# Gated delta recurrence: the keys' roots on ScalarE's logarithm and exponential, the convolution's first product from SBUF

## The chip, the cores and the metric

The kernel runs on one core of a Trainium2 chip. The metric is the device time of one execution in microseconds (us); of several runs the median is taken. The engines of the core work side by side, each through its own list of instructions in order: TensorE (PE, matrix products; PEld is its weight load), VectorE (DVE), ScalarE (ACT), GpSimd (POOL) and SyncE (SP, which issues most of the DMA transfers). They wait for each other through semaphores. SBUF is the memory on the chip, and PSUM the small memory that TensorE writes its products to.

## What is computed

The reference is two transformer blocks one after the other, in float32, on 512 tokens of width 1024. The change touches the second block's gated delta network, in which queries and keys are brought to length one behind a convolution of five taps and a SiLU:

```python
def _gdn_inputs(qkv, beta_logit, decay_logit, conv_w, a_log, dt_bias):
    qkv = jax.nn.silu(_centred_conv(qkv, conv_w))
    ...
    q = _l2norm(q.reshape(B, T, GDN_HEADS, GDN_DK))
    k = _l2norm(k.reshape(B, T, GDN_HEADS, GDN_DK))
```

A recurrence in chunks of 128 tokens follows, forward and backward, over 256 context tokens and the 512 tokens themselves (six chunks), for 8 heads of width 128. Beside it the block has a latent attention (MLA), whose latents are a product of the same input, and an MLP.

## The kernel before

Float32 products are made from three matmuls of high and low parts (`mm3s`, L234, L235 and L237: high by high, low by high, high by low). `weights()` loads a chunk of weights of 512 KB (tile `wraw`), from which ScalarE makes the high part `whi` (L178) and VectorE the low part `wlo` (L179); the three names share six buffers. Products of the projections go to a PSUM bank of the group `pg`, of which there are two.

`gdn()` works through four pairs of heads. For each pair:

- `inputs(pair)` projects keys and queries. `conv()` takes each product out of its PSUM bank twice on ScalarE: L1247 copies it to `raw`, and L1248 writes it, scaled by the middle tap, to `acc`. VectorE adds the other four taps (L1254), and ScalarE applies the Silu (L1256). Each head's keys are turned (TensorE L1284, ScalarE L1286), and ScalarE squares them and sums (L1309, tile `kss`). GpSimd adds 1e-6 (L1312, tile `kn`), raises to the power -1/2 (L1314) and multiplies (L1315): the root of the keys' squared length, `krt`.
- `values(pair)` does the same for the values and scales them by `krt` as they leave PSUM (L1289).
- `betas(pair)` takes the logarithm of `kn` on ScalarE (L1344, tile `kln`) and its reciprocal on VectorE (L1346).
- `within(pair)` makes the matrices inside a chunk: TensorE L1368 to L1378, Exps on ScalarE (L1380), VectorE L1382 to L1384, and copies to the tile `inv` (L1388, L1390).
- `states(pair)` inverts them. VectorE transposes all blocks (L1398), eliminates (L1406, L1409) and transposes back (L1411 for one half, L1412 for the other). TensorE then puts larger blocks together (L1426 to L1466; ScalarE copies in L1437), and six steps of the recurrence follow (L1472 to L1535).
- `output(pair)` norms the result, multiplies it by a gate (Silu L1543, L1560) and stores it by a DMA that ScalarE issues (L1561).

In the code, `inputs`, `values`, `betas` and `within` of the next pair stand behind `states` of this one, and behind the last pair's `states` the products of the MLA latents (`tail()`: three chunks of 256, 256 and 192 columns, taken out of PSUM by L980). A scheduler orders the instructions of TensorE, ScalarE, VectorE and GpSimd when the kernel is built, so work of the next pair, or of the tail, is placed among the steps and the inversion of this one. SyncE keeps the written order. The scheduler's result depends on the whole program: a change of a few instructions can move others.

Of the kernel before, what the change touches and what calls it, by code (L numbers as in the profile page):

```python
# [10 lines left out]
F32 = mybir.dt.float32  # L11
F32R = mybir.dt.float32r
BF = mybir.dt.bfloat16
AF = mybir.ActivationFunctionType
OP = mybir.AluOpType
# [60 lines left out]
class Kernel:  # L76
# [1155 lines left out]
    def gdn(self, H, HC, w, tail):  # L1232
        nc, ap = self.nc, self.ap
        mm, act, dve = nc.tensor.matmul, nc.scalar.activation, nc.vector
        con = self.const
        sel, cw, onw, ones, idb, msk = self.sel, self.convw, self.onw, self.ones, self.idb, self.msk
        X, L, Y = (self.hb.tile([128, 32, 32], F32, name="inv", tag=f"inv{k}") for k in range(3))
        tm = [con.tile([128, 136], F32, name=f"invt{v}") for v in range(2)]
        nc.gpsimd.memset(X, 0.0)

        def conv(ps, tile):

            raw, acc = (self.page([sum(p.shape[1] for p in ps)]) for _ in range(2))
            o = 0
            for p in reversed(ps):
                n = p.shape[1]
                act(raw[:, o:o + n], p, AF.Copy)  # L1247
                act(acc[:, o:o + n], p, AF.Copy, scale=cw[:, 48 + tile:49 + tile])  # L1248
                for i in (0, 1, 3, 4):
                    wi = cw[:, 24 * i + tile:24 * i + tile + 1]  # L1250
                    a, b = max(0, 2 - i), min(n, n + 2 - i)
                    y = acc[:, o + a:o + b]
                    v = raw[:, o + a + i - 2:o + b + i - 2]
                    dve.scalar_tensor_tensor(y, v, wi, y, op0=OP.mult, op1=OP.add)  # L1254
                o += n
            act(acc, acc, AF.Silu)  # L1256
            return acc, raw

        def product(W, X, f, n, tag):
            ps = self.bank([128, n], tag)  # L1260
            self.mm3s(ps, [[v[:, f * 128:f * 128 + 128] for v in W[k]] for k in range(8)], X)
            return ps

        def ahead(f0):

            W = self.weights(w, 0, 8, f0, 256)
            return W, [product(W, HC, f, 256, "sc") for f in range(2)]

        def feat(f0, both, first=None):

            W, pc = first or (None, None)
            W = W or self.weights(w, 0, 8, f0, 256)
            for f in range(2):
                r = [product(W, H, f, 512, "pg")]
                if both:
                    r.append(pc[f] if pc else product(W, HC, f, 256, "pg"))
                yield r

        def turn(src, dst, scale=None):

            for a, m in ((0, 4), (4, 2)):
                pt = self.bank([128, m, 128], "pt")
                for t in range(m):
                    nc.tensor.transpose(pt[:, t], src[:, (a + t) * 128:(a + t) * 128 + 128], self.ident)  # L1284
                if scale is None:
                    act(dst[:, a:a + m], pt, AF.Copy)  # L1286
                    continue
                for t in range(m):
                    act(dst[:, a + t], pt[:, t], AF.Copy, scale=scale[:, a + t:a + t + 1])  # L1289
# [3 lines left out]
        def inputs(pair):  # L1293


            h0 = 2 * pair
            qT, sq_, kT, ktok = ([] for _ in range(4))
            fk = fv = None
            if pair == 0:
                fv = None, ahead(2048)[1]  # L1300
                fk = ahead(1024)
            kc = [conv(ps, 8 + h0 + f) for f, ps in enumerate(feat(1024 + pair * 256, True, fk))]
            n2, root = [], []
            for f, (c, raw) in enumerate(kc):
                kt = self.page([6, 128])
                turn(c, kt)
                ss = self.tmp.tile([128, 6], F32, name="kss")
                for t in range(6):
                    act(raw[:, t * 128:t * 128 + 128], kt[:, t], AF.Square, accum_out=ss[:, t:t + 1])  # L1309
                n2.append(self.hb.tile([128, 6], F32, name=f"kn2{f}", bufs=2))  # L1310
                root.append(self.hb.tile([128, 6], F32, name=f"krt{f}", bufs=2))
                nc.gpsimd.tensor_scalar(n2[f], ss, 1e-6, None, op0=OP.add)  # L1312
                r = self.hb.tile([128, 6], F32, name="krs", bufs=2)
                nc.gpsimd.tensor_tensor(r, n2[f], self.mhalf[:, :6], op=OP.pow)  # L1314
                nc.gpsimd.tensor_tensor(root[f], r, n2[f], op=OP.mult)  # L1315
                kT.append(c.rearrange("p (a b) -> p a b", a=6))
                ktok.append(kt)
            qc = [conv(ps, h0 + f) for f, ps in enumerate(feat(pair * 256, False))]
            for q, sq in qc:
                qT.append(q)  # L1320
                act(sq, q, AF.Square)
                pq = self.bank([128, 4], "pt")
                for t in range(4):
                    mm(pq[:, t:t + 1], sq[:, t * 128:t * 128 + 128], ones, start=True, stop=True)
                s1 = self.tmp.tile([128, 4], F32, name="qss")
                dve.tensor_copy(s1, pq)
                sq_.append(self.rstd(s1, 1.0 / 128, 128e-6, "qrs"))
            return (qT, kT, ktok), (root, sq_), n2, fv

        def values(pair, root, fv):  # L1330

            vtok = []
            for f, ps in enumerate(feat(2048 + pair * 256, True, fv)):
                c, _ = conv(ps, 16 + 2 * pair + f)
                vt = self.page([6, 128])
                turn(c, vt, root[f])
                vtok.append(vt)
            return vtok

        def betas(pair, n2):  # L1340
            h0, nb, bd = 2 * pair, [], []
            for f in range(2):
                ln = self.hb.tile([128, 6], F32, name="kln", bufs=2)
                act(ln, n2[f], AF.Ln)  # L1344
                inv = self.hb.tile([128, 6], F32, name="kin", bufs=2)
                dve.reciprocal(inv, n2[f])  # L1346
                for out, nm, v, op in ((nb, "nb", ln, OP.subtract), (bd, "bd", inv, OP.mult)):
                    out.append(self.hb.tile([128, 6, 2], F32, name=f"k{nm}{f}", bufs=2))
                    dve.tensor_tensor(out[f], g[nm][:, :, h0 + f::8], v[:, :, None].to_broadcast([128, 6, 2]), op=op)
            return nb, bd  # L1350

        D2 = range(2)
# [210 lines left out]

        gg = self.gdn_gates(H, HC, w)
        keys, rest, n2, fv = inputs(0)
        next(gg)
        vtok = values(0, rest[0], fv)
        next(gg)
        g = next(gg)
        nb, bd = betas(0, n2)  # L1570
        EM = within(0, *keys[:2], nb)
        for pair in range(4):
            O = states(pair, *keys, vtok, bd, *EM)
            sq_ = rest[1]
            if pair < 3:
                keys, rest, n2, fv = inputs(pair + 1)
                vtok = values(pair + 1, rest[0], fv)
                nb, bd = betas(pair + 1, n2)
                EM = within(pair + 1, *keys[:2], nb)
            else:  # L1580
                tail()
            output(pair, O, sq_)
# [54 lines left out]
```

## Time and profile before

| | us |
|---|---|
| median of 3 runs | 2291.25 (2290.05 to 2291.55) |
| the profiled execution | 2289.66 |
| its span | 2287.8 |
| TensorE busy | 2185.6 (96%) |
| VectorE busy | 1186.6 (52%) |
| ScalarE busy | 1019.1 (45%) |
| GpSimd busy | 259.3 (11%) |

The busy shares are means over the whole span. TensorE is idle for some 100 us in all, so it is the first engine to look at, and the question is at which places it waits and for whom. The granted clock is TensorE's, as a share of full speed; its mean was 0.984. The recurrence with its inputs and the tail fills the stretch from about 940 to 1460 us. In the timelines a row is one instruction, or several of a kind in a row (xN): its start, its duration, its engine, line and operation, what it writes and reads, and in brackets how long its engine had been idle before it and who released it.

### The profile page before, as it was taken

The page shows a single profiled execution, that of the slowest core. Times are in us where ns is not written, and L with a number is a line of the kernel's source. Part 1 is how long each engine was busy: PE and PEld are TensorE (multiplying, and loading weights), DVE is VectorE, ACT ScalarE, POOL GpSimd, SP SyncE. Part 2 cuts the span into 40 slices and gives each one's busy share as a digit, 9 for nine tenths or more (in the row PEclk, how much of TensorE's full clock was granted, in tenths as well). Part 3 has the DMA queues.
Part 4 walks back from the last instruction along what each step waited for, and adds up shares of the span by engine and source line. Part 5 has one row for each costly group of instructions (what it writes and reads, how often), then busy time and mean ns, then how long its engine had stood idle before and what let it go on. Part 6 is the DMA issues. An engine that isn't in the chain of part 4 may idle for free. (4 is left out here: it accounts for less than half of the span.)

```text
span 2287.8 us, 38189 instructions
## 1 busy us (share of the span) xinstructions
PE 2185.6 (96%) x15367; PEld 1938.3 (85%) x15367; DVE 1186.6 (52%) x2636; ACT 1019.1 (45%) x2072; POOL 259.3 (11%) x411
## 2 busy tenths in 40 slices
PE   7999999998999999998999998999999998999999
PEld 7888988888889889877787888789998797898988
DVE  3554453656443233558687875337774444424333
ACT  4443333545443223566665664446554224314231
POOL 0220100001000001203121211201110011010102
PEclk9999999999999999999999998999999998999999
DMA  5134476455773233522222110331013442223222
GB/s 169 65 115 145 156 245 225 153 184 177 256 248 105 90 102 102 165 81 66 74 66 79 61 56 16 98 117 34 30 38 111 166 144 78 93 90 95 93 92 102
DMA packets 195816, 262.05 MB, mean 115 GB/s; under 512 B 12343, under 2 KB 157495, under 8 KB 195639
## 3 DMA queue, kind: packets, MB, share of 16 engines
q1 hardware_dynamic: 188864, 244.61, 33.1%
q10 hardware_dynamic: 6775, 15.00, 1.7%
q8 instruction: 121, 1.98, 0.3%
q14 instruction: 56, 0.46, 0.1%
HBM read 223.39 MB, written 36.18 MB: 113 GB/s over the span
## 5 line engine op out<-in xcount | busy, mean ns | idle before, releaser
L179 DVE TENSOR_TENSOR wlo<-wraw,whi 128x1024 fp32r<-128x1024 f32 (+2 forms) x267 | 321.7, 1205 | 415.9 <-PE pg L235 213.4
L178 ACT ACTIVATE whi<-wraw 128x1024 fp32r<-128x1024 f32 (+2 forms) x267 | 276.8, 1037 | 443.6 <-DMA wraw<-in_w_mlp_out 96.2
L234 PE MATMUL pg<-xhi,whi 128*128 128x512 f32 (+1 forms) x1104 | 429.4, 391 | 26.7 <-ACT a L1248 15.9
L235 PE MATMUL pg<-xlo,whi 128*128 128x512 f32 (+1 forms) x1104 | 425.4, 388 | 0.0
L237 PE MATMUL pg<-xhi,wlo 128*128 128x512 f32 (+1 forms) x1104 | 293.7, 385 | 2.6 <-DVE wlo L179 2.6
L234 PEld LDWEIGHTS pg<-xhi,whi 128*128 128x128 f32 x1104 | 210.8, 191 | 74.8 <-ACT a L1248 18.1
L235 PEld LDWEIGHTS pg<-xlo,whi 128*128 128x128 f32 x1104 | 210.8, 191 | 37.1
L237 PEld LDWEIGHTS pg<-xhi,wlo 128*128 128x128 f32 x1104 | 203.1, 190 | 41.7 <-DVE wlo L179 3.3
L234 PE MATMUL pg<-whi,xhi 128*128 128x256 f32 (+1 forms) x608 | 160.5, 294 | 3.3 <-ACT whi L178 2.5
L235 PE MATMUL pg<-whi,xlo 128*128 128x256 f32 (+1 forms) x608 | 156.6, 288 | 0.0
L234 PE MATMUL sc<-whi,a 128*128 128x256 f32 x560 | 140.8, 283 | 1.6 <-ACT whi L178 1.6
L234 PE MATMUL pg<-whi,a 128*128 128x256 f32 x560 | 140.9, 283 | 0.5 <-DVE a L148 0.5
L235 PE MATMUL sc<-whi,a 128*128 128x256 f32 x560 | 141.1, 284 | 0.0
L235 PE MATMUL pg<-whi,a 128*128 128x256 f32 x560 | 140.8, 283 | 0.0
L234 PEld LDWEIGHTS pg<-whi,xhi 128*128 128x128 f32 x608 | 118.7, 195 | 10.2 <-ACT whi L178 4.4
L235 PEld LDWEIGHTS pg<-whi,xlo 128*128 128x128 f32 x608 | 118.2, 195 | 1.1 <-issue 0.8
L234 PEld LDWEIGHTS sc<-whi,a 128*128 128x128 f32 x560 | 107.4, 192 | 2.0 <-ACT whi L178 1.8
L234 PEld LDWEIGHTS pg<-whi,a 128*128 128x128 f32 x560 | 107.5, 192 | 0.9 <-DVE a L148 0.9
L1254 DVE SCALAR_TENSOR_TENSOR a<-a,convw,a 128x511 f32<-128x511 f32 (+3 forms) x160 | 97.7, 638 | 20.1 <-ACT a L1248 19.2
L235 PEld LDWEIGHTS sc<-whi,a 128*128 128x128 f32 x560 | 107.5, 192 | 0.2
L929 POOL TENSOR_TENSOR a<-a,a 128x256 f32<-128x256 f32 x64 | 48.8, 763 | 519.5 <-DVE a L928 518.8
L235 PEld LDWEIGHTS pg<-whi,a 128*128 128x128 f32 x560 | 107.5, 192 | 0.0
(475 smaller groups left out, 4570.4 us busy)
## 6 DMA issues: line engine op xcount, KB each, us to landing
wraw<-in_w_in SPq DMA_DIRECT2D x56, 512.0 KB
fraw<-in_w_mod SPq DMA_DIRECT2D x48, 512.0 KB
parts<-fraw SPq DMA_DIRECT2D x48, 512.0 KB
wraw<-in_w_gate_up SPq DMA_DIRECT2D x44, 512.0 KB
wraw<-in_w_mlp_in SPq DMA_DIRECT2D x32, 512.0 KB
wraw<-in_w_mlp_out SPq DMA_DIRECT2D x32, 512.0 KB
whi<-parts SPq DMA_DIRECT2D x26, 512.0 KB
wlo<-parts SPq DMA_DIRECT2D x26, 512.0 KB
```

Source lines behind the costliest of these rows:

```text
L178: nc.scalar.activation(hi, raw, AF.Copy)
L179: self.wlo_eng.tensor_tensor(lo, raw, hi.bitcast(F32), op=OP.subtract)
L234: mm(out, A[k][0], B[k][0], start=start and k == 0, stop=False)
L235: mm(out, A[k][late], B[k][1 - late], start=False, stop=False)
L237: mm(out, A[k][1 - late], B[k][late], start=False, stop=stop and k == n - 1)
L929: nc.gpsimd.tensor_tensor(self.x[t][:, cs], self.x[t][:, cs], u, op=OP.add)
L1254: dve.scalar_tensor_tensor(y, v, wi, y, op0=OP.mult, op1=OP.add)
```

## The change

`conv()` makes the second eviction from `raw` in SBUF and not from PSUM, so that the bank is free after the first. The three GpSimd instructions on the keys of each head go; instead ScalarE takes one logarithm for both heads of a pair, with 1e-6 as its bias, and the exponential of half of it, which is the root. `betas()` uses the same logarithm; VectorE adds 1e-6 and takes the reciprocal of both heads at once. From L1241 on lines of the kernel after stand up to three further down: L1247 and L1248 are L1250 and L1251 there, the keys' Ln and Exp are L1315 and L1317, and the lines from L1348 on keep their numbers.

```diff
+        eps = con.tile([128, 1], F32, name="keps")
+        nc.gpsimd.memset(eps, 1e-6)
...
                 act(raw[:, o:o + n], p, AF.Copy)
-                act(acc[:, o:o + n], p, AF.Copy, scale=cw[:, 48 + tile:49 + tile])
+                act(acc[:, o:o + n], raw[:, o:o + n], AF.Copy, scale=cw[:, 48 + tile:49 + tile])
...
-            n2, root = [], []
+            ss = self.hb.tile([128, 2, 6], F32, name="kss", bufs=2)
...
-                ss = self.tmp.tile([128, 6], F32, name="kss")
                 for t in range(6):
-                    act(raw[:, t * 128:t * 128 + 128], kt[:, t], AF.Square, accum_out=ss[:, t:t + 1])
-                n2.append(self.hb.tile([128, 6], F32, name=f"kn2{f}", bufs=2))
-                root.append(self.hb.tile([128, 6], F32, name=f"krt{f}", bufs=2))
-                nc.gpsimd.tensor_scalar(n2[f], ss, 1e-6, None, op0=OP.add)
-                r = self.hb.tile([128, 6], F32, name="krs", bufs=2)
-                nc.gpsimd.tensor_tensor(r, n2[f], self.mhalf[:, :6], op=OP.pow)
-                nc.gpsimd.tensor_tensor(root[f], r, n2[f], op=OP.mult)
+                    act(raw[:, t * 128:t * 128 + 128], kt[:, t], AF.Square, accum_out=ss[:, f, t:t + 1])
...
+            ln = self.hb.tile([128, 2, 6], F32, name="kln", bufs=2)
+            act(ln, ss, AF.Ln, bias=eps)
+            root = self.hb.tile([128, 2, 6], F32, name="krt", bufs=2)
+            act(root, ln, AF.Exp, scale=0.5)
...
-                turn(c, vt, root[f])
+                turn(c, vt, root[:, f])
...
+            ss, ln = n2
+            inv = self.hb.tile([128, 2, 6], F32, name="kin", bufs=2)
+            dve.tensor_scalar(inv, ss, 1e-6, None, op0=OP.add)
+            dve.reciprocal(inv, inv)
             for f in range(2):
-                ln = self.hb.tile([128, 6], F32, name="kln", bufs=2)
-                act(ln, n2[f], AF.Ln)
-                inv = self.hb.tile([128, 6], F32, name="kin", bufs=2)
-                dve.reciprocal(inv, n2[f])
```

ScalarE in pair 0's inversion, where the second head of pair 1's keys is squared; before:

```order
L1309 ACTIVATE a_10907,kss<-a_10987 128x128 x6
L1344 ACT_TABLE_LOAD
L1344 ACTIVATE kln<-kn_11005 128x6
L1247 ACTIVATE a_11068<-pg 128x512
L1248 ACTIVATE a_11069<-pg,convw 128x512
L1247 ACTIVATE a_11102<-pg 128x512
L1248 ACTIVATE a_11103<-pg,convw 128x512
```

and after:

```order
L1311 ACTIVATE a_10895,kss<-a_10976 128x128 x6
L1250 ACTIVATE a_11047<-pg 128x512
L1251 ACTIVATE a_11048<-a_11047,convw 128x512
L1250 ACTIVATE a_11081<-pg 128x512
L1251 ACTIVATE a_11082<-a_11081,convw 128x512
```

The logarithm no longer stands between the squares and the evictions of the queries' banks; it and the exponential have moved behind the first of the recurrence's steps.

ScalarE ahead of and in pair 3's inversion (its first copy out of the inverse is L1437, the chunks of the latents' weights are L178); before:

```order
L1380 ACTIVATE w_14071<-pt,knb_13975 128x128 x2
L178 ACTIVATE whi<-wraw 128x1024
L1380 ACTIVATE w_14050<-sc,knb_13975 128x128 x4
L1380 ACTIVATE w_14072<-sc,knb_13975 128x128 x4
L1543 ACT_TABLE_LOAD
L1543 ACTIVATE a_14157<-pg 128x512
L1388 ACTIVATE inv<-w_14063 32x192 x4
L1561 DMA od<-a_14130 128x512
L1561 DMA od<-a_14157 128x512
L178 ACTIVATE whi<-wraw 128x1024 x2
L980 ACTIVATE a_14845<-pg 128x256
```

and after:

```order
L1543 ACT_TABLE_LOAD
L1543 ACTIVATE a_14076<-pg 128x512
L1380 ACT_TABLE_LOAD
L1380 ACTIVATE w_13996<-sc,knb_13921 128x128 x4
L1380 ACTIVATE w_14018<-sc,knb_13921 128x128 x4
L1388 ACTIVATE inv<-w_14009 32x192 x4
L1543 ACT_TABLE_LOAD
L1543 ACTIVATE a_14103<-pg 128x512
L1561 DMA od<-a_14076 128x512
L178 ACTIVATE whi<-wraw 128x1024
L1561 DMA od<-a_14103 128x512
L178 ACTIVATE whi<-wraw 128x1024 x2
```

The chunk of weights that stood among the Exps now stands behind them, one Silu stands between the Exps, and no L980 comes before L1437.

TensorE where pair 3's inverses come out (L1426 is its first product with them); before:

```order
L234 MATMUL pg<-whi,xhi 128x256
L235 MATMUL pg<-whi,xlo 128x256
L237 MATMUL pg<-wlo,xhi 128x256 x8
L1426 MATMUL sc<-inv,w_14006 32x32
L1426 MATMUL sc<-inv,w_14063 32x32
L234 MATMUL pg<-whi,xhi 128x256
L1426 MATMUL sc<-inv,w_14028 32x32
```

and after:

```order
L237 MATMUL pg<-wlo,xhi 128x256 x4
L234 MATMUL pg<-whi,xhi 128x256
L235 MATMUL pg<-whi,xlo 128x256
L234 MATMUL pg<-whi,xhi 128x256
L235 MATMUL pg<-whi,xlo 128x256
L234 MATMUL pg<-whi,xhi 128x256
L1426 MATMUL sc<-inv,w_13952 32x32
L1426 MATMUL sc<-inv,w_14009 32x32
```

The rows look alike, but they are other products: between the last product of `within` (L1378) and L1426 there are 168 of the latents' matmuls before and 49 after.

## Rows read from the trace of the kernel before

**Rows 1.** Windows, one inversion each: length, then busy us by engine, clock, DMA.

```profile
1028.07:1061.02 32.95, 25.03 (x126) 20.64 (x124) 32.95 (x139) 13.64 (x34) 14.77 (x8) 0.90 0.34 112
1135.48:1162.41 26.93, 23.07 (x122) 19.43 (x121) 26.89 (x132) 5.25 (x11) 0.01 (x1) 1.00 0.38 126
1245.06:1271.99 26.93, 22.13 (x118) 18.62 (x117) 26.89 (x132) 5.13 (x11) 0.01 (x1) 1.00 0.41 128
1354.29:1381.04 26.75, 19.28 (x144) 18.61 (x144) 26.68 (x127) 4.21 (x9) 0.02 (x1) 0.89 0.13 39
```

**Rows 2.** Windows ahead of pair 2's inversion and behind the last recurrence (PE, PEld, DVE, ACT, POOL).

```profile
1209.40:1245.06 35.66, 35.33 (x187) 27.72 (x186) 23.54 (x46) 25.46 (x62) 4.39 (x4) 1.00 0.35 111
...
1420.00:1430.00 10.00, 10.00 (x87) 10.00 (x86) 1.58 (x2) 1.37 (x5) 0.12 (x1) 1.00 0.05 8
...
1450.00:1460.00 10.00, 6.03 (x26) 4.43 (x27) 3.38 (x7) 8.25 (x24) 6.06 (x13) 1.00 0.22 79
```

**Rows 3.** TensorE's waits from 940 to 1460: us in total, times, longest.

```profile
PE pg L234 <- ACT a L1248: 15.9, 8, 6.9
```

**Rows 4.** Timelines of GpSimd, ScalarE, TensorE and VectorE in pair 0's inversion.

```profile
1038.20 11.18 POOL L1312 TENSOR_SCALAR kn<-kss 128x6 f32<-128x6 f32 x1 [52.50 <-ACT a L1309]
...
1049.41 0.21 ACT L1344 ACTIVATE kln<-kn 128x6 f32<-128x6 f32 x1 [10.00 <-POOL kn L1312]
...
1050.74 0.79 PE L234 MATMUL pg<-xhi,whi 128*128 128x512 f32 x1 [6.86 <-ACT a L1248]
...
1058.28 2.04 DVE L1412 STREAM_TRANSPOSE inv<-inv 128x1024 f32<-128x1024 f32 x1
...
1061.02 0.98 PE L1426 MATMUL sc<-inv,w 32*32 32x32 f32 x84
```

**Rows 5.** Timelines of ScalarE and TensorE at the wait ahead of the first inversion.

```profile
1000.64 0.66 ACT L1247 ACTIVATE a<-pg 128x512 f32<-128x512 f32 x1
1001.12 0.76 ACT L1248 ACTIVATE a<-pg,convw 128x512 f32<-128x512 f32 x1
...
1001.93 0.80 PE L234 MATMUL pg<-xhi,whi 128*128 128x512 f32 x1 [4.31 <-ACT a L1248]
```

**Rows 6.** Timeline of TensorE, products of 256 and of 512 columns back to back.

```profile
1419.76 0.28 PE L234 MATMUL pg<-whi,xhi 128*128 128x256 f32 x1
...
1420.72 0.64 PE L237 MATMUL pg<-wlo,xhi 128*128 128x256 f32 x4
...
1446.97 0.39 PE L235 MATMUL pg<-xlo,whi 128*128 128x512 f32 x1
...
1448.58 1.07 PE L237 MATMUL pg<-xhi,wlo 128*128 128x512 f32 x4
```

**Rows 7.** Timelines of VectorE and TensorE at the ends of the other inversions.

```profile
1162.16 1.99 DVE L1412 STREAM_TRANSPOSE inv<-inv 128x1024 f32<-128x1024 f32 x1
...
1162.41 0.28 PE L1426 MATMUL sc<-inv,w 32*32 32x32 f32 x4 [2.06 <-DVE inv L1411]
...
1271.99 0.28 PE L1426 MATMUL sc<-inv,w 32*32 32x32 f32 x4 [3.13 <-DVE inv L1411]
...
1377.87 1.43 PE L237 MATMUL pg<-wlo,xhi 128*128 128x256 f32 x8 [3.99 <-DVE wlo L179]
1381.04 0.39 PE L1426 MATMUL sc<-inv,w 32*32 32x32 f32 x4 [1.73 <-DVE inv L1411]
```

**Rows 8.** Timeline of VectorE, low parts of the latents' weights around pair 3's inversion.

```profile
1346.77 1.22 DVE L179 TENSOR_TENSOR wlo<-wraw,whi 128x1024 fp32r<-128x1024 f32 x1 [0.53 <-ACT whi L178]
...
1376.59 1.23 DVE L179 TENSOR_TENSOR wlo<-wraw,whi 128x1024 fp32r<-128x1024 f32 x1
```

**Rows 9.** Timeline of ScalarE, a switch of tables ahead of pair 2's inversion.

```profile
1230.54 1.28 ACT L1380 ACT_TABLE_LOAD   x1
1231.83 1.14 ACT L1380 ACTIVATE w<-pt,knb 128x128 f32<-128x128 f32 x4
```

**Rows 10.** Window of the 8 us from the end of pair 3's inversion on.

```profile
1380.00:1388.00 8.00, 4.94 (x243) 4.42 (x245) 5.78 (x9) 5.47 (x16) 3.58 (x8) 0.50 0.10 32
```

More of the change, by code (lines that the diff above doesn't have):

```diff
@@ L1327, in inputs @@
                 sq_.append(self.rstd(s1, 1.0 / 128, 128e-6, "qrs"))
-            return (qT, kT, ktok), (root, sq_), n2, fv
+            return (qT, kT, ktok), (root, sq_), (ss, ln), fv
         def values(pair, root, fv):
@@ L1341, in betas @@
             h0, nb, bd = 2 * pair, [], []
+            ss, ln = n2
+            inv = self.hb.tile([128, 2, 6], F32, name="kin", bufs=2)
+            dve.tensor_scalar(inv, ss, 1e-6, None, op0=OP.add)
+            dve.reciprocal(inv, inv)
             for f in range(2):
-                ln = self.hb.tile([128, 6], F32, name="kln", bufs=2)
-                act(ln, n2[f], AF.Ln)
-                inv = self.hb.tile([128, 6], F32, name="kin", bufs=2)
-                dve.reciprocal(inv, n2[f])
                 for out, nm, v, op in ((nb, "nb", ln, OP.subtract), (bd, "bd", inv, OP.mult)):
                     out.append(self.hb.tile([128, 6, 2], F32, name=f"k{nm}{f}", bufs=2))
-                    dve.tensor_tensor(out[f], g[nm][:, :, h0 + f::8], v[:, :, None].to_broadcast([128, 6, 2]), op=op)
+                    dve.tensor_tensor(out[f], g[nm][:, :, h0 + f::8], v[:, f, :, None].to_broadcast([128, 6, 2]), op=op)
             return nb, bd
```

## The prediction

> **What bounds the kernel now.** The changed lines all lie in the recurrence, some 500 us of 2290. I read the busy shares by stretch first, then TensorE's waits, then the timelines of the engines around the longest wait.
>
> The recurrence runs through four pairs of heads, and each pair has one stretch in which TensorE isn't the engine that sets the end. [Rows 1] show it: from L1398 (VectorE's first transposition of a pair's matrices) to L1426 (TensorE's first product with their inverses) VectorE is busy for the whole 27 to 33 us, without a hole. TensorE is busy for 19 to 25 us of them, with products that have nothing to do with the inversion: the next pair's projections, and for the last pair the latents of the attention that follows. I call these products **fill**. Outside these stretches TensorE hardly stops: 35.33 of 35.66 us ahead of pair 2's inversion, 10.00 of 10.00 behind the last recurrence [rows 2]. So time is won where fill that ran elsewhere moves into an inversion that had an idle TensorE, and lost where fill is taken out of one.
>
> The largest wait for the two ops that the change touches is TensorE's for L1248, the scaled copy out of PSUM: 15.9 us in 8 places [rows 3]. The longest of them shows what the change aims at [rows 4]: GpSimd's add L1312 takes 11.18 us while VectorE inverts, ScalarE stands at the Ln behind it until 1049.41, its evictions come after that, and TensorE restarts at 1050.74 after 6.86 us. But this wait lies inside pair 0's inversion. VectorE's L1412 ends at 1060.32 all the same, and TensorE reaches L1426 at 1061.02, 0.70 us later.
>
> **The change part by part.**
>
> *Roots and logarithms.* GpSimd loses three instructions a head, 24 in all. ScalarE has 8 Ln before, and 4 Ln and 4 Exp after. The wait on GpSimd is gone, since the squares' sums are now ScalarE's own results. In pair 0's inversion TensorE's fill therefore ends some 7 us earlier, and TensorE then waits for L1411 and L1412, which VectorE computes without a hole. Half of L1426's products need L1411 alone and could begin before L1412's end, as pair 1's do (at 1162.41, with L1412 from 1162.16 to 1164.15) [rows 7]; the other half can't. So the chain can gain the 0.70 us by which TensorE came late, and no more. I take 0 and keep -0.7 as the end.
>
> *The convolution's first product.* The bank is released by the plain copy. Seven waits remain, 9.0 us in all. In the order after, the plain copies stand ahead of the scaled ones where two banks are emptied, so each of these waits shrinks by a copy or vanishes; but six of them share 4.7 us and lie where fill runs or in the inversions. The longest, of 4.31 us ahead of the first inversion lies on the path: its product starts 0.05 us after a scaled copy of 0.76 us [rows 5]. That one copy is what it saves, and perhaps an overlap of 0.2 more: **-0.8 us** (0 to -1). The scaled copy itself reads SBUF and follows its own engine's copy; no row shows that form. The nearest rows are the two copies out of PSUM, 0.66 us plain and 0.76 us scaled [rows 5], so I bound it at 0.1 us either way. VectorE's taps behind it belong to the next pair and lie beside TensorE's fill, so I count 0.
>
> *The order.* The scheduler places everything anew, and this is the larger part. I counted, in the orders of both kernels, TensorE's instructions between the last L1378 ahead of an inversion (which VectorE's L1398 needs) and the first L1426. Of the projections' products with 512 columns, pairs 0 to 3 have 96, 99, 93 and 1 before, and 90, 106, 107 and 7 after: **21 more**. Eight of them start 0.23 us apart ((1448.58 - 1446.97) / 7) [rows 6]. There is room for them: pairs 1 and 2 end with waits of 2.06 and 3.13 us for L1411 [rows 7], and pair 0's six fewer run ahead of it instead, which the sum has as a loss of 1.4. That gives 21 x 0.23 = **-4.8 us**.
>
> Of the latents' products with 256 columns the last inversion had 168 and has **49** now; the other pairs keep their 48. The reason is one chunk of weights. Before, ScalarE made its high part (L178) among the Exps ahead of the inversion, and VectorE its low part (L179) at 1346.77, so that two chunks were ready when the inversion began and the third came at 1376.59 [rows 8]. In the order after, no L179 of the latents stands ahead of L1398: the first follows it directly, and the second stands where the one of 1376.59 stands, at the inversion's end. TensorE thus stops after some 40 products until about 23 us into the inversion, although the high parts are there. The other 119 run behind the recurrence, where TensorE is back to back. Eight of them take 0.96 us (1420.72 - 1419.76) [rows 6], so they cost 119 x 0.12 = **+14.3 us**. VectorE's count of instructions inside the inversion is the same, so L1411 comes no later.
>
> Part of the 14.3 may be paid by idle time that follows: TensorE is busy for 6.03 of 10 us at 1450 to 1460 [rows 2], where it waits for weights and for VectorE's norms. These follow from TensorE's own latents and so move with them; I take -0.7 of the 4.0 that are there.
>
> *ScalarE's tables.* The order has 51 table loads in place of 49: the keys' eight stay eight (an Ln and an Exp for each pair), two are saved elsewhere, and the stretches ahead of the inversions of pairs 2 and 3 each get two more, since the Silu of the output's gate now stands between the Exps. A switch costs 1.28 us and nothing besides: the Exp starts 1.29 us after the load [rows 9]. ScalarE has room there (25.46 of 35.66 us busy ahead of pair 2's inversion), TensorE has not [rows 2], so I take 0 and keep 4 x 1.28 = +5.1 as the end. The Trainium skill (ScalarE: Activation LUTs, What ACT_TABLE_LOAD costs) gives 1.283 us for the load and some 1.38 us more for draining the engine at each switch; by it the end would be 10.6 us. The trace agrees with the first figure and shows no room for the second: the load's own row is followed by its Exp 0.01 us later.
>
> *Sum:* -0.8 - 4.8 + 14.3 - 0.7 = **+8.0 us**. Against the profiled execution's 2289.66 that is 2297.7; against the median of the runs, 1.6 above it, **2299**. A measurement of this kernel tells 0.2% (4.6 us) from no change.
>
> **The rivals.**
>
> *A, faster: the 119 products cost nothing.* The recurrence of pair 3 and what follows would have to hold enough idle time on TensorE to take them. Then -0.8 - 4.8 = -5.6 stays: 2285.6. It decides from where less than 1 us of the 14.3 remains. Against it: 10.00 of 10.00 us at 1420 to 1430. For it: the recurrence is a chain through three engines, and a stretch in which TensorE only looks busy, because matmuls wait in its pipe, wouldn't show.
>
> *B, no difference: the stalls count in full.* If TensorE's position in the order and not VectorE's inversion set the recurrence's start, all 15.9 us of waits would come back and pay for the 14.3: 2289.7. Against it: [rows 1 and 4].
>
> *C, no difference: the idle time after the recurrence takes its 4.0 us in full*, and pair 0's end its 0.7: 2299.3 - 3.3 - 0.7 = 2295.3, just inside the 4.6.
>
> *D, slower by more: the table switches lie on the path.* ScalarE's Exps are what L1388 and so the inversion wait for. If the four switches show, 2299.3 + 5.1 = 2304.4. A colder TensorE would add to it: the granted clock was 0.50, the lower of its two levels, in the 8 us after the last inversion, where TensorE had waited 3.99 and 1.73 us [rows 7, 10]. In the order after it waits longer there, and for some 5 us at the end of pair 0's inversion too. The recurrence's first products are small, so I count up to 1 us.
>
> *E: the change doesn't do what it says.* The evictions could wait behind the Silu instead. In pair 0's inversion that costs nothing, as there are some 5 us to spare, so the time would be the forecast's.
>
> **How the numbers follow.** The forecast with E 0.42 and D 0.13 make slower 0.55. C 0.16 and B 0.11 make no difference 0.27. A 0.14, and 0.04 for gains that I haven't seen, make faster 0.18. The range goes from A's neighbourhood, 2286, which leaves out some 0.14, to 2305, a little past D. The forecast's own range without the other cases is 2295 to 2304.
>
> **What would show it.** In the profile after, no wait for GpSimd on ScalarE, and the waits of TensorE for the convolution's copies down from 15.9 us to under 5. Pair 0's inversion still takes 32 us, and its L1426 waits for L1411 for 4 us or more. Pairs 1 and 2 wait less than 2 us each there. In pair 3's inversion TensorE idles for 15 us or more before an L237 that waits for L179, and the stretch from L1426 to the latents' last product is some 14 us longer. I am wrong if pair 3's inversion shows TensorE busy for 19 us as before, if the inversions themselves get shorter, or if the latents end no later, counted from L1426.

## The result, and the profile after

The changed kernel runs in 2302.38 us (median of 4, 2301.03 to 2309.55) against 2290.65 us for the kernel before in the same comparison: 1.0060 times its time, with a 95% interval of 1.0039 to 1.0081, or 11.7 us slower. On another chip the ratio was 1.0048 (1.0036 to 1.0060). The profiled execution after took 2303.49 us, with a span of 2300.9. The kernel before itself took between 2288 and 2303 us on the chips of the experiments, so the experiments below are told by their ratio to it on the same chip.

The waits of TensorE after the change, in total, times and the longest, from 940 to 1480 us; they answer to [rows 3]:

```profile
PE pg L237 <- DVE wlo L179: 18.2, 3, 13.7
PE sc L1426 <- DVE inv L1411: 15.2, 4, 9.1
PE pg L234 <- ACT whi L178: 7.1, 4, 3.6
PE pg L234 <- ACT a L1250: 3.2, 1, 3.2
```

The wait for the convolution's copies, the first in [rows 3], is down from 15.9 to 3.2 us, and no engine waits for GpSimd's root any more. What has come in its place stands above it. The four inversions after the change, by window (length, then the busy time of PE, PEld, DVE, ACT and POOL, the granted clock, DMA); they answer to [rows 1]:

```profile
1032.01:1062.31 30.30, 21.24 (x115) 18.14 (x114) 30.30 (x137) 9.98 (x25) 0.01 (x1) 0.92 0.37 122
1141.50:1168.41 26.91, 24.52 (x131) 20.90 (x130) 26.88 (x132) 6.86 (x13) 0.01 (x1) 1.00 0.45 147
1247.78:1274.67 26.89, 24.05 (x129) 20.52 (x128) 26.86 (x132) 6.86 (x13) 0.01 (x1) 1.00 0.44 148
1359.35:1386.02 26.67, 10.20 (x49) 9.43 (x48) 26.60 (x128) 2.23 (x3) 0.02 (x1) 0.56 0.10 30
```

VectorE again fills each of them, and they are as long as before but for pair 0's, whose L1426 starts at the end of L1411 now. In pairs 1 and 2 TensorE does more (24.52 for 23.07, 24.05 for 22.13 us). In pair 3 it does 10.20 us of work where it did 19.28. Its timeline there, and VectorE's low parts of the weights:

```profile
1358.57 0.58 PE L234 MATMUL pg<-whi,xhi 128*128 128x256 f32 x1 [3.61 <-ACT whi L178]
1362.48 1.22 PE L237 MATMUL pg<-wlo,xhi 128*128 128x256 f32 x4 [1.84 <-DVE wlo L179]
1382.84 1.22 PE L237 MATMUL pg<-wlo,xhi 128*128 128x256 f32 x4 [13.74 <-DVE wlo L179]
1386.02 0.39 PE L1426 MATMUL sc<-inv,w 32*32 32x32 f32 x4 [0.89 <-DVE inv L1411]
...
1361.23 1.20 DVE L179 TENSOR_TENSOR wlo<-wraw,whi 128x1024 fp32r<-128x1024 f32 x1
1381.57 1.22 DVE L179 TENSOR_TENSOR wlo<-wraw,whi 128x1024 fp32r<-128x1024 f32 x1
```

No L179 of the latents precedes the inversion (1359.35), the second comes 22 us into it, and TensorE stands for 13.74 us. The products that didn't run there run behind the recurrence. Where TensorE turns the last blocks of the latents' normed columns, its timeline has, before and after:

```profile
1472.56 0.66 PE L1005 MATMUL pt<-ident,a 128*128 128x128 f32 x4 [0.43 <-DVE ckv L151]
```

```profile
1491.54 0.66 PE L1005 MATMUL pt<-ident,a 128*128 128x128 f32 x4 [0.42 <-DVE ckv L151]
```

From pair 3's L1426 that is 1472.56 - 1381.04 = 91.52 us before and 1491.54 - 1386.02 = 105.52 after: 14.0 us longer. But the span has grown by 13.1 us only, so other parts pay some of it back. The parts are: 3.9 us up to the first L1398 (1028.07 to 1032.01), 1.1 from there to pair 3's L1398, -0.1 in pair 3's inversion, 14.0 to the row above, and **-5.8 from there to the end**, in code that the change doesn't touch. The first part is of the size by which kernels with one and the same order differ (with the order of the change the first L1398 stood at 1032.01, 1032.58 and 1035.68, with before's order at 1026.33, 1028.07, 1030.54 and 1033.30), and I read nothing from it. The last one I did not expect.

### The profile page after: what moved, and what is told of

It reads as the page before. It is cut to its first block, busy times and chain, and to the rows that moved or that the text cites. A ratio compares the mean times of both kernels' runs of the same rounds, so it can differ in the third digit from the quotient of the medians.

```text
span 2300.9 us, 38162 instructions
## 1 busy us (share of the span) xinstructions
PE 2186.8 (95%) x15367; PEld 1938.2 (84%) x15367; DVE 1186.3 (52%) x2636; ACT 1024.6 (45%) x2074; POOL 230.0 (10%) x388
## 5 line engine op out<-in xcount | busy, mean ns | idle before, releaser
L179 DVE TENSOR_TENSOR wlo<-wraw,whi 128x1024 fp32r<-128x1024 f32 (+2 forms) x267 | 321.6, 1205 | 427.2 <-PE pg L235 229.4
L178 ACT ACTIVATE whi<-wraw 128x1024 fp32r<-128x1024 f32 (+2 forms) x267 | 276.8, 1037 | 472.0 <-DMA wraw<-in_w_mlp_out 110.7
L237 PE MATMUL pg<-xhi,wlo 128*128 128x512 f32 (+1 forms) x1104 | 294.0, 386 | 3.4 <-DVE wlo L179 3.4
L237 PEld LDWEIGHTS pg<-xhi,wlo 128*128 128x128 f32 x1104 | 202.8, 190 | 42.1 <-DVE wlo L179 4.1
L234 PE MATMUL sc<-whi,a 128*128 128x256 f32 x560 | 138.4, 280 | 1.6 <-ACT whi L178 1.6
L235 PE MATMUL sc<-whi,a 128*128 128x256 f32 x560 | 138.7, 280 | 0.0
L237 PE MATMUL pg<-wlo,xhi 128*128 128x256 f32 (+1 forms) x608 | 103.2, 291 | 15.6 <-DVE wlo L179 15.6
L234 PEld LDWEIGHTS pg<-whi,a 128*128 128x128 f32 x560 | 105.0, 188 | 1.0 <-DVE a L148 0.9
L235 PEld LDWEIGHTS pg<-whi,a 128*128 128x128 f32 x560 | 105.2, 188 | 0.0
```

The source lines that it names most:

```text
L178: nc.scalar.activation(hi, raw, AF.Copy)
L179: self.wlo_eng.tensor_tensor(lo, raw, hi.bitcast(F32), op=OP.subtract)
L234: mm(out, A[k][0], B[k][0], start=start and k == 0, stop=False)
L235: mm(out, A[k][late], B[k][1 - late], start=False, stop=False)
L237: mm(out, A[k][1 - late], B[k][late], start=False, stop=stop and k == n - 1)
```

## The experiments

**One part of the change at a time.** The convolution alone is the kernel before with one line:

```diff
-                act(acc[:, o:o + n], p, AF.Copy, scale=cw[:, 48 + tile:49 + tile])
+                act(acc[:, o:o + n], raw[:, o:o + n], AF.Copy, scale=cw[:, 48 + tile:49 + tile])
```

> Only the convolution's part of the change: the scaled copy reads SBUF; the keys' roots stay on GpSimd. Theory (fill): its order keeps 167 of the latents' matmuls in pair 3's inversion (168 before, 49 after the whole change), and has 8 projections' matmuls more in the inversions, 8 x 0.23 = 1.8 us. So about 2288, 2 to 3 us faster than before; pair 3's inversion has TensorE busy for some 19 us. Rival (the convolution itself costs): a second copy that reads SBUF behind the first makes VectorE's taps late, and the time goes up by several us although the fill is there.

Measured: 0.9979 (0.9967 to 0.9992), 4.8 us faster than before. Pair 3's inversion in its trace:

```profile
1359.16:1385.80 26.64, 19.84 (x140) 19.25 (x139) 26.57 (x127) 4.21 (x9) 0.01 (x1) 0.87 0.14 39
```

TensorE is busy for 19.84 us of it, about as in [rows 1] (19.28). The second copy from SBUF costs nothing that shows.

The other part alone is the changed kernel with that line turned back.

> Only the roots' part: logarithm and exponential on ScalarE, both evictions of the convolution still from PSUM. Theory (fill): its order has 49 of the latents' matmuls in pair 3's inversion, like the whole change, and 8 projections' matmuls more in the others: +14.3 - 1.8, about 2303, and TensorE idle for some 14 us before an L237 in pair 3's inversion. Rival (the loss is the convolution's): no slower than before.

Measured: 1.0077 (1.0054 to 1.0100), 17.7 us slower. TensorE in pair 3's inversion:

```profile
1388.23 1.22 PE L237 MATMUL pg<-wlo,xhi 128*128 128x256 f32 x4 [15.00 <-DVE wlo L179]
1391.45 0.39 PE L1426 MATMUL sc<-inv,w 32*32 32x32 f32 x4 [0.92 <-DVE inv L1411]
...
1497.23 0.66 PE L1005 MATMUL pt<-ident,a 128*128 128x128 f32 x4 [0.42 <-DVE ckv L151]
```

The idle time is there, and L1426 to L1005 takes 105.78 us. So the lost fill comes with the roots. It was 5.7 us more than expected, and this stays open. Its trace has the loss in two stretches: from pair 0's L1398 to pair 1's it took 110.77 us (107.41 before), and from pair 1's to pair 2's 115.25 (109.58).

**The fill given back.** The whole change, with the first chunk of the latents' weights marked as urgent for the scheduler (`f0 == 0` is that chunk):

```diff
+            with self.tc.high_priority() if f0 == 0 else ExitStack():
-            W = self.weights(w, 0, 8, 4128 + f0, fn)
+                W = self.weights(w, 0, 8, 4128 + f0, fn)
```

> The whole change, and the first chunk of the latents' weights marked urgent for the scheduler (its copies L178 and L179 come as early as they can). Nothing else is edited; the order again has 168 of the latents' matmuls in pair 3's inversion, and the same 16 more projections' matmuls in the other inversions. Theory (fill): some 14 us less than the whole change, about 2288. Rival (tables and roots cost by themselves): the four more table switches and the two instructions on ScalarE stay, so the time stays above 2297.

Measured: 0.9978 (0.9963 to 0.9993), 5.0 us faster than before, and so some 16 to 19 us faster than the whole change (1.0048 to 1.0060); the profiled spans differ by 11.1 us. Pair 3's inversion, and TensorE behind the latents (L1006 is L1005 there; pair 3's L1426 starts at 1388.04):

```profile
1362.20:1388.04 25.84, 16.06 (x126) 15.59 (x125) 25.74 (x127) 3.54 (x9) 0.01 (x1) 0.81 0.18 50
```

```profile
1479.64 0.66 PE L1006 MATMUL pt<-ident,a 128*128 128x128 f32 x4 [0.42 <-DVE ckv L151]
```

The stretch from L1426 to this row takes 91.60 us again. The 14 us are the fill's, shown by taking it away (the roots' part) and by giving it back with the roots in place.

**The cold clock.** In the changed kernel TensorE waits 9.06 us at the end of pair 0's inversion, and the granted clock is 0.50 behind it. The whole change with 30 useless matmuls there:

```diff
+                if pair == 0 and j == 18:
+                    key = self.hb.tile([128, 128], BF, name="warmk")
+                    dve.tensor_copy(key, Y[:, 0:4].rearrange("p a b -> p (a b)"))
+                    spare = self.bank([128, 4, 128], "sc")
+                    for i in range(30):
+                        mm(spare, key, msk[:, 0, None, :].to_broadcast([128, 4, 128]), start=True, stop=True)
```

> The whole change, and 30 matmuls more on TensorE whose results nobody reads, placed at the end of pair 0's inversion, where it waits 9 us in the profile after. They wait for a copy that VectorE makes in the middle of the inversion (one instruction, about 0.2 us). Theory (cold clock): the granted clock was 0.50 there until 9 us after the inversion; with TensorE kept busy it stays at 1.00, and the stretch from L1426 to the next L1398 goes from 79.2 us to the 74 to 75 of before, so the run is 4 us faster than the whole change, about 2298, although more is computed. Rival (order): the 4.7 us that this stretch has lost come from waits of the new order, and it stays at 79.

Measured: 1.0029 (1.0013 to 1.0045), 6.7 us slower than before: 4 to 7 us less than the whole change. The 12 us from 1062 on, of the whole change and of this kernel (windows as above):

```profile
1062.00:1068.00 6.00, 3.77 (x192) 3.40 (x198) 5.86 (x10) 5.64 (x16) 5.04 (x10) 0.50 0.02 4
1068.00:1074.00 6.00, 6.00 (x163) 5.44 (x158) 4.61 (x8) 5.75 (x15) 1.00 (x4) 0.73 0.02 5
```

```profile
1062.00:1068.00 6.00, 3.73 (x121) 3.14 (x115) 5.10 (x10) 4.62 (x13) 2.10 (x6) 0.89 0.02 5
1068.00:1074.00 6.00, 5.56 (x71) 5.03 (x67) 2.64 (x6) 4.61 (x15) 0.00 (x0) 0.83 0.00 1
```

These are the same times, not the same places: pair 0's L1426 starts at 1062.31 in the whole change and at 1057.41 here. In the three windows of 6 us from L1426 on, the clock was 0.50, 0.75 and 1.00 in the whole change, and 1.00, 0.77 and 0.94 here. So it was higher, but it fell for a while here too. The stretch that the expectation names, from L1426 to the next L1398, took 77.4 us, between the 79.2 of the whole change and the 74.5 of before. From pair 0's L1398 to pair 1's it is 107.2 us, 109.5 in the whole change, and 107.4 before. So the clock's price there is about 2 us, less than half of the 4.7 that I had put on it, and uncertain: two more kernels with the order of the change (the first two in the next part) took 112.2 and 108.6 us. The rest of the run's gain is not in this stretch: from pair 2's L1398 to pair 3's it took 109.0 us where the whole change took 111.6, with the same order and the same waits before L1426 (2.85 and 0.36 us against 2.84 and 0.36). The difference is the clock again, which was 0.51 and 0.50 in the windows from 1276 to 1288 of the whole change:

```profile
1276.00:1282.00 6.00, 4.53 (x249) 4.29 (x250) 4.36 (x11) 4.96 (x15) 3.65 (x7) 0.51 0.03 7
1282.00:1288.00 6.00, 5.78 (x91) 4.99 (x87) 4.97 (x9) 4.94 (x11) 1.00 (x4) 0.50 0.01 3
```

In the first three windows of 6 us from L1426 on it was 0.62, 0.50 and 0.74 there, and 0.72, 1.00 and 1.00 in the kernel with the useless matmuls. The two more kernels with the order of the change took 112.2 and 110.6 us for this stretch, and the given-back chunk 111.2. So the longer stretch comes again, and the 109.0 us are the odd ones; why the clock was back sooner in that execution stays open.

**The 5.8 us behind the latents.** In that stretch the MLP's matmuls of 256 columns take less time after the change. Their groups before and after, between 1960 and 2250 us (busy time, mean ns of one, idle before; the window catches fewer of them after the change, since they run later there):

```profile
L234 PE MATMUL pg<-whi,a 128*128 128x256 f32 x210 | 52.7, 283 | 0.0
```

```profile
L234 PE MATMUL pg<-whi,a 128*128 128x256 f32 x192 | 47.3, 279 | 0.0
```

Where they follow one another without a hole (1916 times), they start 0.1200 us apart before and 0.1178 after, by the start times in the traces; the expectations below have 0.1195 and 0.1177. That is 4.2 of the 5.8 us. The convolution's part alone has 283, the roots' part alone, the given-back chunk and the useless matmuls have 279, on one and the same chip, so it belongs to the program.

The other 1.6 us are a sum of two things. The branches' products, 512 columns wide, become slower. Their group between 1700 and 1900 us, before and after:

```profile
L235 PE MATMUL pg<-a,whi 128*128 128x512 f32 x128 | 49.8, 389 | 0.0
```

```profile
L235 PE MATMUL pg<-a,whi 128*128 128x512 f32 x128 | 50.5, 394 | 0.0
```

They start 0.2267 us apart before and 0.2334 after, and their stretch grows by 1.8 us (87.8 to 89.6). The convolution's part alone has 389 ns too, so this follows the program in the same way. The MLP's products of 512 columns, which stand between those of 256, take 3.0 us less (197.9 to 194.9). This doesn't go with the 279 ns: the convolution's part alone has 194.7 us, the roots' part alone 198.1.

For the 256-column matmuls my first theory was the new tile for 1e-6: it moves the weights' buffers and the pages of activations by 32 bytes, off the multiples of 64. Four kernels on one chip, the whole change first:

> The whole change once more, on the chip of the next three runs, for comparison with them: 0.6% slower than before, as measured, and 256-column matmuls of the MLP of 279 ns in its trace (283 before).

Measured: 1.0048 (1.0036 to 1.0060), and 279 ns.

```diff
-        eps = con.tile([128, 1], F32, name="keps")
+        eps = con.tile([128, 16], F32, name="keps")
-            act(ln, ss, AF.Ln, bias=eps)
+            act(ln, ss, AF.Ln, bias=eps[:, :1])
```

> The whole change, with the tile that holds 1e-6 64 bytes long in each partition instead of 32. The orders of TensorE, ScalarE and VectorE are the same as after the change, row by row; what differs is that the weights' buffers, the activations and the pages lie at multiples of 64 bytes, as before the change, and not 32 bytes beside them. Theory (addresses): the 32 bytes made the 256-column matmuls of the MLP start 0.1177 us apart and not 0.1195; at multiples of 64 they take 283 ns in the trace again, and the run is 5 us or more slower than the whole change (6432 such matmuls x 0.0018 us = 11.6 at most, 5.8 by the stretch behind the latents). Rival (execution): the spacing belongs to the execution and not to the program; no difference to the whole change.

Measured: 1.0053 (1.0040 to 1.0066), and 279 ns: no difference to the whole change.

```diff
+        eps = con.tile([128, 1], F32, name="keps")
+        nc.gpsimd.memset(eps, 1e-6)
```

> The kernel before with nothing but an unused tile of 32 bytes (set once by GpSimd), which moves the weights' buffers, the activations and the pages off the multiples of 64 bytes. The order of its instructions is that of before. Theory (addresses): 279 ns for the MLP's 256-column matmuls, and 5 to 11 us less than before, about 2283. Rival (execution): the time of before.

Measured: 0.9999 (0.9990 to 1.0008), and its group:

```profile
L234 PE MATMUL pg<-whi,a 128*128 128x256 f32 x203 | 50.9, 283 | 0.0
```

The convolution's part with the same unused tile:

> Only the convolution's part of the change, and the unused tile of 32 bytes. Theory (fill and addresses): the gain of the convolution's part alone (0.2% as measured) and that of the 32 bytes add up: 0.4 to 0.6% faster than before, the fastest of these kernels. Rival (execution): no faster than the convolution's part alone.

Measured: 0.9980 (0.9969 to 0.9991), and 283 ns: the gain of the convolution's part and nothing more. That theory fell: moving the buffers and the pages by 32 bytes together doesn't matter. But the rival, that the spacing belongs to the execution, fell too. What the 283 kernels share is the distance from the weights' buffers to the pages, which the built programs state: 129920 - 25472 = 104448 bytes in each partition, or 51 x 2048 (the buffers are 4 KB and the pages 2 or 4 KB long, so every such pair is a multiple of 2048 apart). The 279 kernels have 104384, since the change takes the tile `kss` out of the pool that lies between the two. The kernel before with that one move:

```diff
-                ss = self.tmp.tile([128, 6], F32, name="kss")
+                ss = self.hb.tile([128, 6], F32, name="kss", bufs=2)
```

> The kernel before, with the tile of the keys' sums (kss) in the pool of the recurrence instead of the general one, as the change has it; the orders of all engines are those of before, row by row. That moves the activations' pages 64 bytes towards the weights' buffers: their distance is 104448 bytes (51 x 2048) before, in the kernel with the unused tile and with the convolution's part alone, which all have 283 ns for the MLP's 256-column matmuls, and 104384 after the change, with 64 bytes for the 1e-6 and with the roots' part alone, which all have 279. Theory (distance): 279 ns, and 6 us or more less than before (5.8 by the stretch behind the latents). Rival (something else that comes with the roots on ScalarE, such as GpSimd's power): 283 ns and the time of before.

Measured: 0.9975 (0.9963 to 0.9987), 5.7 us faster than before, and its group:

```profile
L234 PE MATMUL pg<-whi,a 128*128 128x256 f32 x207 | 51.0, 279 | 0.0
```

The convolution's part with it:

> The convolution's part alone (0.2% faster than before) with the keys' sums moved in the same way. Theory (distance): 279 ns, and the two gains add up to 0.4 to 0.5%, the fastest of these kernels. Rival (something else): 283 ns and 0.2%.

Measured: 0.9954 (0.9941 to 0.9967), 10.6 us faster than before: the two gains add up, and it is the fastest of all these kernels against its own before. The distance the other way, from before, with an unused tile in the pool between:

```diff
+        far = self.tmp.tile([128, 16], F32, name="far", bufs=1)
+        nc.gpsimd.memset(far, 1e-6)
```

> The kernel before, with an unused tile of 64 bytes in the general pool; the order of the instructions is that of before. It moves the activations' pages 64 bytes away from the weights' buffers: a distance of 104512 bytes, where 104448 (51 x 2048) gave 283 ns for the MLP's 256-column matmuls and 104384 gave 279. Theory (104448 is the odd one, since it is a multiple of 2048): 279 ns, and some 6 us less than before. Rival (only the smaller distance is fast): 283 ns and the time of before.

Measured: 0.9963 (0.9947 to 0.9980), 8.5 us faster than before, and its group:

```profile
L234 PE MATMUL pg<-whi,a 128*128 128x256 f32 x219 | 54.1, 281 | 0.0
```

The mean length of a row, 281 ns, misleads here. By their starts these matmuls follow each other every 0.1169 us, closer than with 279 ns, and their four stretches in the MLP take 222.1 us in sum, against 223.8 in each kernel with 279 and 228.0 in each with 283. The branches' products start 0.2290 us apart. So of three distances the multiple of 2048 bytes is the slow one for the 256-column matmuls, but the fast one for the branches' products. Three points don't make a rule, and why it is so no trace here shows.

## Why the prediction was right

The forecast was +8.0 us, the measured difference 11.7 (11.0 by the ratio on the other chip), and it lies in the range of 2286 to 2305. The sign came from one term, and that term held. That the size came so close is luck: another term of the sum failed, and some 5.7 us that the prediction doesn't have paid for it.

- **The 119 latents' products, +14.3.** Measured +14.0 (105.52 against 91.52 us), by a wait of 13.74 us in front of the L237 that the prediction named. Rival A, that they cost nothing, fell, and rival C too: the wait for the next weights behind them is still 2.21 us where it was 2.35, so it moved with the latents and paid back nothing of the 0.7 that I took for it.
- **Projections into the inversions, -4.8.** From pair 1's L1398 to pair 2's, 106.28 us against 109.58, or -3.3; TensorE's instructions between pair 1's L1426 and the end of pair 2's `within` are 15 fewer in the order, 15 x 0.23 = 3.5. From pair 2's to pair 3's the like 14 are -3.2 by count, and the stretch is 2.3 us longer instead. This is the step that failed; from pair 0's L1398 to pair 3's the forecast had -4.8, and +1.1 was measured. It turned a count into time as if TensorE set the end of each such stretch. From pair 2's L1426 to pair 3's L1398, before, after and in the kernel with the useless matmuls (windows as above):

```profile
1271.99:1354.29 82.30, 78.69 (x807) 67.95 (x808) 58.42 (x133) 68.69 (x190) 18.21 (x32) 0.98 0.13 43
1274.67:1359.35 84.68, 77.14 (x775) 66.97 (x776) 57.15 (x131) 68.33 (x188) 13.78 (x26) 0.91 0.09 27
1269.39:1351.51 82.12, 73.77 (x775) 63.78 (x776) 57.02 (x131) 68.19 (x188) 13.77 (x26) 0.97 0.09 27
```

TensorE's work went down, with a clock near that of before by 4.9 us, but its idle time rose from 3.6 to 8.4 us (7.5 after the change), and the end came no earlier. 3.61 us of it are the wait for L178 ahead of pair 3's inversion, shown above, while ScalarE works without a hole (see the tables below): in that last piece ScalarE's chain sets L1398. This is read from the rows; no run tests it. The waits for L1411 did not shrink below 2 us (2.40 and 2.84), because the waits for the copies inside the same inversions went as well and left their time there.
- **The cold clock, counted at 1 us at most.** It was mis-sized: about 2 us in pair 0, by the run with useless matmuls, and 1.6 to 3.2 behind pair 2's inversion, by three executions with the order of the change against that run.
- **The tables, taken as 0 with an end of 5.1.** Between 1340 and 1354 us ScalarE works without a hole, and the Exps of pair 3 stand behind a switch there and back. ScalarE's timeline after:

```profile
1347.69 1.13 ACT L1380 ACTIVATE w<-pt,knb 128x128 f32<-128x128 f32 x4
1348.84 1.28 ACT L1543 ACT_TABLE_LOAD   x1
1350.13 0.60 ACT L1543 ACTIVATE a<-pg 128x512 f32<-128x512 f32 x1
1350.73 1.28 ACT L1380 ACT_TABLE_LOAD   x1
1352.03 2.17 ACT L1380 ACTIVATE w<-sc,knb 128x128 f32<-128x128 f32 x8
```

From the end of the last L1378 to L1398 it is 1359.35 - 1352.46 = 6.9 us, and 1354.29 - 1348.29 = 6.0 before. So about 0.9 of rival D shows here. The rows also settle what the Trainium skill (ScalarE: Activation LUTs, What ACT_TABLE_LOAD costs) would have added for a drain at each switch: each load starts at most 0.02 us behind the row before it and is followed by its function 0.01 or 0.02 us later, and the switch there and back costs 2 x 1.28 and no more.
- **The convolution's copies, -0.8.** The wait ahead of the first inversion fell from 4.31 to 3.18 us, and the others, but for this one, are gone. Rival B, that all 15.9 would come back, fell with L1426's wait of 9.06 us in pair 0: the stall under GpSimd's add really did lie beside VectorE's inversion. E was not needed.
- **Not in the prediction at all: some -5.7** from the distance of two buffers, as measured by the kernel before with `kss` moved. Behind the latents this is -4.2 + 1.8; another -3.1 lies in the first block, where 1411 matmuls of the same form (`whi,a` and `wlo,a`) start 0.1199 us apart before and 0.1177 after. Without it the change would cost some 17 us, an estimate from these two ratios, and the time would be 2308, outside the range. The remaining -3.0 behind the latents, in the MLP's 512-column products, comes with the convolution's part. The roots' part alone has the 279 ns too and still costs 17.7, so the convolution's part, worth 4.8 us alone, is in the whole change as well.

The price of the roots on ScalarE itself, with the fill right and the distance the same, is the difference between the given-back chunk (0.9978) and the convolution's part with `kss` moved (0.9954), on one chip: 0.24%, or 5.5 us. In their profiles 4.3 of it lie between pair 2's L1398 and pair 3's (111.18 and 106.91 us), where the former has the colder clock and the additional switches. How the two share it I can't tell. In this kernel no run shows a gain from the move off GpSimd: it freed time inside a stretch that VectorE sets.

## What to carry to other kernels

Before counting a wait as a gain, find the stretch that contains it, and ask which engine sets that stretch's end: 6.86 us of TensorE idling under VectorE's inversion were worth nothing. Where a scheduler orders the program, count in the new order how much independent work each such stretch still holds; a chunk of weights that slips past its start cost 14 us here, and marking it urgent brought them back. When code that a change doesn't touch gets faster or slower, compare the buffers' addresses too, and go by the start times of the matmuls and not by the mean length of their rows: a tile of 24 bytes that moved from one pool to another was worth 5.7 us.

## What the hardware showed beside this

TensorE's rate depended on where its two operands lay to each other. In the MLP's 256-column matmuls the weights' buffers hold the moving operand, and the pages the 128x128 operand that is loaded. With the two 104448 bytes apart, these matmuls took 283 ns in the trace and started 0.1200 us apart; at 104384 it was 279 ns and 0.1178, and at 104512 281 ns and 0.1169, all at a granted clock of 1.00 and with the order of the instructions unchanged. In the branches' 512-column products the pages hold the moving operand; they started 0.2267, 0.2334 and 0.2290 us apart at the same three distances, so there the first is the fastest. The Trainium skill (SBUF — State Buffer, SBUF: two separate sides) says that TensorE's ports never wait for anyone, and (Who interferes with whom) that its reads of the moving operand and of the weights are independent; the measured 5.7 us for an edit that moved addresses alone don't fit that as it stands. Which two accesses get in each other's way, no run here shows.

The granted clock stayed at its lower level after similar waits for different times. TensorE waited 2.8 to 3.0 us at the end of pair 2's inversion in four executions with the same order there. In the three windows of 6 us that followed, the clock was 0.62, 0.50 and 0.74 in the whole change, 0.64, 0.50 and 0.72 when it ran again, 0.72, 0.85 and 0.86 with the longer tile for 1e-6, and 0.72, 1.00 and 1.00 with the useless matmuls in pair 0.
